# A conditioned two-layer decoder trunk on one core: the first phase with modulation columns by products that take the data as weights, and another order of its steps

## The chip, the cores and the metric

One Trainium2 chip, one of its cores. A core has engines that each work through their own queue in order and wait for one another by semaphores: TensorE (PE, with its weight loads shown apart as PEld), VectorE (DVE), ScalarE (ACT), GpSimd (POOL), and SyncE (SP), which here only issues DMAs. The metric is the device time of one execution in microseconds; the median of the runs counts.

## The reference, cut to what matters

Two layers; the first phase of the kernel computes the first lines of layer 0: the modulation of the six vectors `sh1 .. g2`, the norm, and the start of the q, k and v products.

```python
cond = jax.nn.silu(c)
for i in range(DEPTH):
    mod = cond @ ada_w[i] + ada_b[i]
    sh1, sc1, g1, sh2, sc2, g2 = [m[:, None, :] for m in jnp.split(mod, 6, axis=-1)]
    h = rms_norm(x, norm_mix[i]) * (1.0 + sc1) + sh1
    if i % N_MIXERS == 0:
        mix = stick_breaking_attention(h, sb_w_in[j], sb_w_out[j])   # qkv = h @ w_in, ...
    else:
        mix = dsa_attention(h, ...)
    x = x + g1 * mix
    h = rms_norm(x, norm_ffn[i]) * (1.0 + sc2) + sh2
    x = x + g2 * conv_ffn(h, ...)
```

D_MODEL is 1024, SEQ 512, BATCH 1, 16 heads of 64 in layer 0. All inputs are float32.

## The kernel before

Activations lie transposed: x and h are eight tiles of 128 features x 512 positions (f = 0 to 7). Each weight product keeps float32 accuracy by splitting both factors into a rounded high part and the rest (`whi`, `wlo` of a weight chunk by `split_hi` on ACT and `split_lo` on DVE; `hhi`, `hlo` of an h tile) and adding three products: hi x hi, weight-lo x hi, hi x lo (`mm3`, L257; PE lines L258 to L260). A weight chunk is 128 x 1024 floats (512 KB); `raws` has six buffers for chunks as they come from memory, and SP issues their loads in the order of the code, each when its buffer is free.

`stick_layer` (L539) begins with a phase written out by hand: the order of the lines in it is the order in each engine's queue. It has these steps.

- Loads: eight x tiles, the small constants `sm`, then for each f two chunks of the modulation weights (`load_ada`, scale first, then shift) between the weight chunks of the first q, k and v products (`FIRST`, L98; `fetch`).
- The norm: squares of the x tiles (ACT, one on DVE), DVE adds some of them, four products with `ones_mean` add over the partitions into `pt_norm` (L589). Then the inverse root on ACT (L679) and one Newton step on DVE (L687 to L689), which leave r.
- The modulation of tile f. For f below `ROWS` (5) `rows(f)` (L597) makes eight products with a 32-column tile of the condition as weights and the modulation weights as moving data (scale and shift together for f below `BOTH`, 3), ACT copies the sums (L608), and `columns(f)` (L610) turns them into columns by products with one moving column (L613). For the others `ada_dot` (L265) multiplies a chunk by the condition, spread over all partitions (`cond`), and sums along the row on DVE (`scale_dot`, `shift_dot`). `cond` comes as a 512 KB broadcast load (L693) and a Silu over it (L726).
- `factor(f)` (L626) adds the scale into `sfac`; `hi_part(f)` (L635) makes u = r * sfac * x on DVE and h's high part on ACT (u + shift); `lo_part(f)` (L640) makes the low part on DVE.
- The first products: `first_part(i, k)` (L661) adds h tile k into group i (q and k of head pairs 0 and 1, tiles `pt_first`), `first_v(k)` (L671) into the value groups (`pt_fv`).
- `keep_busy(n)` (L565) issues n products whose sums nobody reads.

After the last tile the q and k sums are copied out (`evac_q`, `evac_k`), and with `scores(0, 0)` (product z, L897) a second part begins in which a loop over heads is filled up with the products of the other chunks (`FILL`, L99).

Of the kernel before, what the change touches and what calls it, by code (L numbers as in the profile page):

```python
# [9 lines left out]
F32 = mybir.dt.float32  # L10
# [122 lines left out]
def kernel_body(ctx, tc, xT, wst, cst, smalls, crow, ccol, relb, outT):  # L133
# [405 lines left out]
    def stick_layer(l):  # L539
        with ExitStack() as st:  # L540
# [3 lines left out]
            head = ap.tile([P, 288], F32, name="head", bufs=1)  # L544
            condz, ccols, ghalf = head[:, :256], head[:, 256:256 + KT], head[:, 264:264 + KT]
            pool.memset(condz, 0.0)
# [3 lines left out]
            nc.sync.dma_start(sm, smalls)  # L550
# [11 lines left out]
            fetch(0)  # L562
            load_ada(1)
            fetch(1)
# [9 lines left out]
            act.activation(condz.rearrange("p (k m) -> p k m", m=32)[:, :, 0], ccols, AF.Silu)  # L574
# [5 lines left out]
            for f in range(KT):  # L580
                if f == 3:
                    dve.tensor_mul(sq[f], x[f], x[f])
                else:
                    act.activation(sq[f], x[f], AF.Square)
                if 2 < f < KT - 1:
                    dve.tensor_add(sq[2], sq[2], sq[f])
            warm(AF.Abs_reciprocal_sqrt)
            for i, f in enumerate((0, 1, KT - 1, 2)):
                pe.matmul(pn, lhsT=ones_mean, rhs=sq[f], start=i == 0, stop=i == 3)  # L589
                if i == 1:  # L590
                    keep_busy(4)
# [5 lines left out]
            def rows(f):  # L597

                pm = parts[f] = ptile([P, S], "pt_m", "tr")
                n = 2 * P if f < BOTH else P  # L600
                for k in range(KT):
                    q = k % 4
                    w = ada_raw[0 if f < BOTH and k >= 4 else 1, f]
                    kk = q if f < BOTH else k
                    pe.matmul(pm[32 * q:32 * q + 32, :n], lhsT=condz[:, 32 * k:32 * k + 32],
                              rhs=w[:, kk * n:(kk + 1) * n], start=k < 4, stop=k >= 4)
                pr = parts[f, "row"] = ap.tile([P, 2 * P], F32, name="pr", tag="m")
                act.activation(pr[:, :n], pm[:, :n], AF.Copy)  # L608

            def columns(f):  # L610
                pm, pr = parts[f], parts.pop((f, "row"))
                for i in range(2 if f < BOTH else 1):
                    pe.matmul(pm[:, 2 * P + i:2 * P + i + 1], lhsT=pr[:, i * P:(i + 1) * P], rhs=ones1, start=True, stop=True)  # L613
# [12 lines left out]
            def factor(f):  # L626

                src = mod[l][:, KT + f:KT + f + 1] if f >= ROWS else parts[f][:, 2 * P:2 * P + 1]
                dve.scalar_tensor_tensor(sfac[:, f:f + 1], src, ghalf[:, f:f + 1], sfac[:, f:f + 1], op0=OP.mult, op1=OP.add)
                if f < BOTH:  # L630
                    dve.tensor_add(mod[l][:, f:f + 1], parts[f][:, 2 * P + 1:2 * P + 2], shift_bias(f))
# [3 lines left out]
            def hi_part(f):  # L635
                us_[f] = ap.tile([P, S], F32, name="u", tag="ohi", bufs=6)
                dve.scalar_tensor_tensor(us_[f], r, sfac[:, f:f + 1], x[f], op0=OP.mult, op1=OP.mult)
                act.activation(hs[f][0], us_[f], AF.Identity, bias=mod[l][:, f:f + 1])

# [6 lines left out]
            def split_first(i):  # L646

                tag = ("at", "a")[i % 2]

                def new(name):  # L650
                    return ap.tile([P, LW], F32R, name=name, tag=tag)[:, :D] if i >= 4 else split_tile(name)

                split_hi(new, 0)
                yield
                split_lo(new)
                cs[i] = chunk(FIRST[i], 0)

            pts = [ptile([P, S], "pt_first", "mm" if i < 3 else "x") for i in range(4)]
            ptv = []

            def first_part(i, k):  # L661
                w = slice(k * P, (k + 1) * P)
                mm3(pts[i], cs[i][0][:, w], cs[i][1][:, w], hs[k][0], hs[k][1], k == 0, k == KT - 1)
# [7 lines left out]
            def first_v(k):  # L671
                if not ptv:
                    ptv.extend(ptile([P, S], "pt_fv", "z") for _ in range(2))
                whi, wlo = cs[4 + k // 4]
                for t in range(QT):
                    v_part(ptv, whi, wlo, k, t)
# [3 lines left out]
            rows(0)  # L680
            keep_busy(2)
            columns(0)
            keep_busy(6)
            s0, s1, s2, s3 = (split_first(i) for i in range(4))
            next(s0)
# [6 lines left out]
            row = crow[0:1, 0:1]  # L692
            nc.sync.dma_start(cond, bass.AP(tensor=row.tensor, offset=row.offset, ap=[[0, P], [1, D]]))  # L693
            factor(0)
            hi_part(0)
            rows(1)
            keep_busy(4)
            next(s0, None)
            load_ada(3)
            lo_part(0)  # L700
            columns(1)
            fetch(4)
            next(s1)
            first_part(0, 0)
            factor(1)
            hi_part(1)
            rows(2)
            next(s1, None)
            fetch(5)
            first_part(1, 0)  # L710
            lo_part(1)
            columns(2)
            next(s2)
            first_part(0, 1)
            first_part(1, 1)
            factor(2)
            hi_part(2)
            next(s2, None)
            lo_part(2)
            first_part(2, 0)  # L720
            first_part(2, 1)
            next(s3)
            next(s3, None)
            load_ada(4)
            nc.sync.dma_start(cons, cst)
            act.activation(cond, cond, AF.Silu)  # L726
            first_part(3, 0)
            first_part(3, 1)
            s4, s5 = split_first(4), split_first(5)
            first_part(0, 2)  # L730
            first_part(1, 2)
            rows(3)
            shift_dot(3)
            load_ada(5)
            next(s4)
            first_part(2, 2)
            columns(3)
            factor(3)
            hi_part(3)
            first_part(3, 2)  # L740
            next(s4, None)
            lo_part(3)
            rows(4)
            first_v(0)
            first_v(1)
            next(s5)
            next(s5, None)
            load_ada(6)
            shift_dot(4)
            load_ada(7)  # L750
            columns(4)
            first_part(0, 3)
            first_part(1, 3)
            for f in range(4, KT - 1):
                factor(f)
                hi_part(f)
                if f == 4:
                    first_part(2, 3)
                    first_part(3, 3)
                shift_dot(f + 1)  # L760
                lo_part(f)
                scale_dot(f + 1)
                if f == 4:
                    first_v(2)
                    first_v(3)
                if f < KT - 2:
                    for i in range(4):
                        first_part(i, f)
                    first_v(f)
            factor(KT - 1)  # L770
            hi_part(KT - 1)
            fetch(7)
            for i in range(2):
                first_part(i, KT - 2)
            lo_part(KT - 1)
# [45 lines left out]
            def evac_q(p, pt):  # L821
# [10 lines left out]
                later(0.8, lo)  # L832

            def evac_k(p, pt):
# [4 lines left out]
                def lo():  # L839
                    for e, t in enumerate(kd):  # L840
                        a = slice(64 * e, 64 * e + 64)
                        dve.tensor_sub(kl[e][a, :], pt[a, :], t[a, :].bitcast(F32))
# [5 lines left out]
                later(1.2, lo)  # L848
# [112 lines left out]
            for i in range(2):  # L961
# [3 lines left out]
            first_v(KT - 2)  # L965
            release(0.8)
            tick(1.4)
            first_v(KT - 1)
# [6 lines left out]
            for i in range(2, 4):  # L975
                first_part(i, KT - 2)
                first_part(i, KT - 1)
                tick(1.4)
            warm(AF.Sigmoid)
# [638 lines left out]
def _pack(i):  # L1618
# [6 lines left out]
    for t in range(ROWS):  # L1625
        if t < BOTH:
            both = np.concatenate([sc[t], sh[t]], axis=2)
            buf[CH["ada", 0, 1, t]] = both[:, :4].reshape(P, D)
            buf[CH["ada", 0, 0, t]] = both[:, 4:].reshape(P, D)
        else:  # L1630
            buf[CH["ada", 0, 1, t]] = sc[t].reshape(P, D)
# [80 lines left out]
```

## Time and profile before

| | us |
|---|---|
| median of 3 runs (lowest, highest) | 1260.68 (1260.23, 1261.4) |
| the profiled execution | 1260.67 |
| its span in the trace | 1258.9 |
| PE busy, share of the span | 1252.2 (99%) |
| DVE busy | 925.9 (74%) |
| ACT busy | 584.6 (46%) |

The times of a row in the timeline are its start and its length in microseconds from the start of the span; "x4" after a row means four instructions put together, and an fp32 product counts as two. What stands in brackets is how long the engine was idle before the row and what it waited for. A matmul's length includes its way through the array, so that neighbouring rows overlap; the distance of their starts is what they cost.

### The profile page before, as it was taken

The page shows a single profiled execution, that of the slowest core. Times are in us where ns is not written, and L with a number is a line of the kernel's source. Part 1 is how long each engine was busy: PE and PEld are TensorE (multiplying, and loading weights), DVE is VectorE, ACT ScalarE, POOL GpSimd, SP SyncE. Part 2 cuts the span into 40 slices and gives each one's busy share as a digit, 9 for nine tenths or more (in the row PEclk, how much of TensorE's full clock was granted, in tenths as well). Part 3 has the DMA queues.
Part 4 walks back from the last instruction along what each step waited for, and adds up shares of the span by engine and source line. Part 5 has one row for each costly group of instructions (what it writes and reads, how often), then busy time and mean ns, then how long its engine had stood idle before and what let it go on. Part 6 is the DMA issues. An engine that isn't in the chain of part 4 may idle for free.

```text
span 1258.9 us, 17379 instructions
## 1 busy us (share of the span) xinstructions
PE 1252.2 (99%) x6562; PEld 1038.0 (82%) x6562; DVE 925.9 (74%) x1573; ACT 584.6 (46%) x1029; POOL 66.1 (5%) x203
## 2 busy tenths in 40 slices
PE   9999999999999999999999999999999999999999
PEld 6888787798888888888887788887988888888887
DVE  5899998878877777885768878887876456456653
ACT  5477666554323423443445346656543234334330
POOL 0100000002000000000002350110000000000000
PEclk9999999999999999999999999999999999999999
DMA  9644444514575575554412222133122422433231
GB/s 376 217 138 133 130 133 141 170 33 141 191 255 189 179 239 192 187 183 155 130 34 68 84 76 75 52 101 105 64 92 75 134 92 68 125 90 95 76 92 67
DMA packets 49252, 163.05 MB, mean 130 GB/s; under 512 B 5632, under 2 KB 6144, under 8 KB 49168
## 3 DMA queue, kind: packets, MB, share of 16 engines
q1 hardware_dynamic: 48736, 161.15, 39.9%
q8 instruction: 52, 0.85, 0.3%
q10 hardware_dynamic: 432, 0.79, 0.2%
q14 instruction: 32, 0.26, 0.1%
HBM read 159.77 MB, written 2.14 MB: 129 GB/s over the span
## 4 chain that ended last, share of the span: by engine, by line
PE 97%; DMA 1%; DVE 1%; ACT 0%; issue 0%; SPq 0%; DVEq 0%
PE pt_u L259 12%; PE pt_u L258 12%; PE pt_u L260 12%; PE pt_d L259 5%; PE pt_d L258 5%; PE pt_d L260 5%; PE pt_l L258 2%; PE pt_q L258 2%; PE pt_l L259 2%; PE pt_l L260 2%; PE pt_q L260 2%; PE pt_q L259 2%; PE pt_first L258 2%; PE pt_first L260 2%; PE pt_first L259 2%; PE pt_qk L258 2%
## 5 line engine op out<-in xcount | busy, mean ns | idle before, releaser
L218 ACT ACTIVATE whi<-raw 128x1024 fp32r<-128x1024 f32 (+1 forms) x206 | 204.9, 1003 | 116.5 <-PE pt_d L260 86.3
L258 PE MATMUL pt_u<-hhi,whi 128*128 128x512 f32 x640 | 249.0, 389 | 0.0
L259 PE MATMUL pt_u<-hhi,wlo 128*128 128x512 f32 x640 | 249.0, 389 | 0.0
L260 PE MATMUL pt_u<-hlo,whi 128*128 128x512 f32 x640 | 249.0, 389 | 0.0
L226 DVE TENSOR_TENSOR wlo<-raw,whi 128x1024 fp32r<-128x1024 f32 (+1 forms) x194 | 223.4, 1154 | 10.0 <-ACT whi L218 9.2
L1031 ACT ACTIVATE y<-pt_u,sm 128x512 f32<-128x512 f32 x80 | 62.1, 777 | 190.6 <-PE pt_u L260 190.6
L258 PEld LDWEIGHTS pt_u<-hhi,whi 128*128 128x128 f32 x640 | 120.1, 188 | 25.0
L260 PEld LDWEIGHTS pt_u<-hlo,whi 128*128 128x128 f32 x640 | 120.1, 188 | 24.9
L259 PEld LDWEIGHTS pt_u<-hhi,wlo 128*128 128x128 f32 x640 | 120.1, 188 | 24.9
L1032 DVE SCALAR_TENSOR_TENSOR y<-pt_u,sm,y 128x511 f32<-128x511 f32 x80 | 59.9, 749 | 98.1 <-ACT y L1031 98.1
L258 PE MATMUL pt_d<-acthi,whi 128*128 128x512 f32 x288 | 112.0, 389 | 0.0
L259 PE MATMUL pt_d<-acthi,wlo 128*128 128x512 f32 x288 | 112.0, 389 | 0.0
L260 PE MATMUL pt_d<-actlo,whi 128*128 128x512 f32 x288 | 112.0, 389 | 0.0
L267 DVE SCALAR_TENSOR_TENSOR raw<-raw,cond 128x1024 f32<-128x1024 f32 x88 | 106.6, 1217 | 1.1 <-DMA raw<-wst 1.1
L385 DVE SCALAR_TENSOR_TENSOR x<-pt_d,mod,x 128x512 f32<-128x512 f32 x48 | 36.0, 750 | 72.8 <-PE pt_d L260 72.8
L242 ACT ACTIVATE acthi<-y 128x512 fp32r<-128x512 f32 x44 | 27.8, 632 | 104.7 <-DVE y L1050 104.7
L258 PE MATMUL pt_first<-hhi,whi 128*128 128x256 f32 (+1 forms) x200 | 64.1, 321 | 0.0
L259 PE MATMUL pt_first<-hhi,wlo 128*128 128x256 f32 (+1 forms) x200 | 62.9, 314 | 0.9 <-DVE wlo L226 0.8
L258 PEld LDWEIGHTS pt_d<-acthi,whi 128*128 128x128 f32 x288 | 54.1, 188 | 11.3
L260 PEld LDWEIGHTS pt_d<-actlo,whi 128*128 128x128 f32 x288 | 54.1, 188 | 11.2
L259 PEld LDWEIGHTS pt_d<-acthi,wlo 128*128 128x128 f32 x288 | 54.1, 188 | 11.2
L260 PE MATMUL pt_first<-hlo,whi 128*128 128x256 f32 (+1 forms) x200 | 63.1, 315 | 0.0
(256 smaller groups left out, 2512.4 us busy)
## 6 DMA issues: line engine op xcount, KB each, us to landing
raw<-wst SPq DMA_DIRECT2D x250, 512.0 KB, 3.7
raw<-wst SPq DMA_DIRECT2D x48, 384.0 KB, 3.0
th<-rb SPq DMA_DIRECT2D x16, 256.0 KB, 3.0
ada<-wst SPq DMA_DIRECT2D x4, 512.0 KB, 6.2
outT<-x SPq DMA_DIRECT2D x7, 256.0 KB, 2.0
x<-xT SPq DMA_DIRECT2D x5, 256.0 KB, 5.1
x<-xT ACTq DMA_DIRECT2D x3, 256.0 KB, 3.9
cond<-crow SPq DMA_DIRECT2D x1, 512.0 KB, 10.2
```

Source lines behind the costliest of these rows:

```text
L218: act.activation(hi[:, :n], raw[:, :n], AF.Copy)
L226: engine.tensor_sub(lo[:, :n], raw[:, :n], hi[:, :n].bitcast(F32))
L242: act.activation(hi, src, AF.Copy)
L258: pe.matmul(out, lhsT=whi, rhs=ahi, start=start, stop=False)
L259: pe.matmul(out, lhsT=wlo, rhs=ahi, start=False, stop=False)
L260: pe.matmul(out, lhsT=whi, rhs=alo, start=False, stop=stop)
L267: dve.scalar_tensor_tensor(raw, raw, 1.0, cond, op0=OP.mult, op1=OP.mult, accum_out=dst)
L385: dve.scalar_tensor_tensor(x[f][:, c], pt, mod[l][:, g * KT + f:g * KT + f + 1], x[f][:, c], op0=OP.mult, op1=OP.add)
L1031: act.activation(y, pt, AF.Identity, scale=cw[2], bias=sm[:, b + S_CB + c:b + S_CB + c + 1])
L1032: dve.scalar_tensor_tensor(y[:, 1:], pt[:, :S - 1], cw[1], y[:, 1:], op0=OP.mult, op1=OP.add)
```

## The change

Only the first phase changes. The core of the diff:

```diff
-FIRST = [("q", 0), ("k", 0), ("q", 1), ("k", 1), ("v", 0, 0), ("v", 0, 1)]
+FIRST = [("v", 0, 0), ("q", 0), ("k", 0), ("q", 1), ("k", 1), ("v", 0, 1)]
-BOTH = 3
-ROWS = 5
+ROWS = 3
...
-            nc.sync.dma_start(sm, smalls)
+            nc.sync.dma_start(sm[:, :S_CW], smalls[:, :S_CW])
+            nc.sync.dma_start(ident, cst[:, C_ID:C_ID + P])
...
             warm(AF.Silu)
-            act.activation(condz.rearrange("p (k m) -> p k m", m=32)[:, :, 0], ccols, AF.Silu)
+            act.activation(csilu, ccols, AF.Silu)
+            warm(AF.Abs_reciprocal_sqrt)
...
-            for i, f in enumerate((0, 1, KT - 1, 2)):
-                pe.matmul(pn, lhsT=ones_mean, rhs=sq[f], start=i == 0, stop=i == 3)
-                if i == 1:
-                    keep_busy(4)
+            def sum_tile(f):
+                pe.matmul(pn, lhsT=ones_mean, rhs=sq[f], start=f == 0, stop=f == 6)
...
+            dve.tensor_tensor(cond.rearrange("p (k m) -> p k m", k=KT), ident[:, None, :].to_broadcast([P, KT, P]),
+                              csilu[:, :, None].to_broadcast([P, KT, P]), op=OP.mult)
...
+            def column(f, g):
+                pm = parts[f, g] = ptile([P, S], "pt_m", "tr")
                 for k in range(KT):
-                    q = k % 4
-                    w = ada_raw[0 if f < BOTH and k >= 4 else 1, f]
-                    kk = q if f < BOTH else k
-                    pe.matmul(pm[32 * q:32 * q + 32, :n], lhsT=condz[:, 32 * k:32 * k + 32],
-                              rhs=w[:, kk * n:(kk + 1) * n], start=k < 4, stop=k >= 4)
+                    pe.matmul(pm[:, :1], lhsT=ada_raw[g, f][:, k * P:(k + 1) * P], rhs=csilu[:, k:k + 1],
+                              start=k == 0, stop=k == KT - 1)
...
+            def shift(f):
+                dve.tensor_add(mod[l][:, f:f + 1], parts[f, 0][:, :1], shift_bias(f))
...
+            def xr_part(f):
+                us_[f] = ap.tile([P, S], F32, name="xr", tag="olo" if f < 6 else "ohi", bufs=6)
+                dve.tensor_mul(us_[f], r, x[f])
+            def hi_both(f):
+                for out in (hs[f][0], us_[f]):
+                    act.activation(out, us_[f], AF.Identity, scale=sfac[:, f:f + 1], bias=mod[l][:, f:f + 1])
+            def lo_sub(f):
+                dve.tensor_sub(hs[f][1], us_.pop(f), hs[f][0].bitcast(F32))
+            def cond_spread():
+                for i in range(2):
+                    cond_pt.append(ptile([P, S], "pt_c", "mm"))
+                    pe.matmul(cond_pt[i], lhsT=ones_mean, rhs=cond[:, i * S:(i + 1) * S], start=True, stop=True)
+            def cond_copy(i):
+                act.activation(cond[:, i * S:(i + 1) * S], cond_pt[i], AF.Copy, scale=float(D))
...
-            rows(0)
-            keep_busy(2)
-            columns(0)
-            keep_busy(6)
...
+            column(0, 1)
+            column(0, 0)
+            cond_spread()
...
-            row = crow[0:1, 0:1]
-            nc.sync.dma_start(cond, bass.AP(tensor=row.tensor, offset=row.offset, ap=[[0, P], [1, D]]))
...
-            act.activation(cond, cond, AF.Silu)
...
-            rows(3)
...
-            rows(4)
...
+            scale_dot(3)
+            lo_sub(2)
...
+            scale_dot(4)
+            xr_part(5)
+            lo_sub(3)
...
-            for i in range(2):
-                first_part(i, KT - 1)
-                later(0.1, lambda i=i: (evac_k if i else evac_q)(0, pts[i]))
-                tick(0.7)
+            first_part(0, KT - 1)
+            evac_q(0, pts[0], True)
+            first_part(1, KT - 1)
+            evac_k(0, pts[1], True)
```

So for tiles 0 to 2 the scale and the shift each come from a `column`: eight products that take a chunk of the modulation weights as stationary data and one column of the condition as moving data. The scales of tiles 3 and 4 come from dots on DVE. `cond` is made on the chip: DVE spreads the condition over a diagonal, two products with `ones_mean` sum it over the partitions into `pt_c`, ACT copies it out. From tile 2 on h is r * x on DVE, then two ACT passes (high part, and the same unrounded), then one subtraction on DVE. The value chunk comes first, the chunk of the next value group is split within the loop, the table loads of the inverse root and of the sigmoid stand earlier, and the idle products behind the first ten are gone.

On PE, from the norm to the first weight product. Before (`pt_idle` is what `keep_busy` writes, `pt_m` the modulation sums, `head` and `ecols` hold the condition and a column of ones, `pr` is ACT's copy of the sums):

```order
L589 MATMUL pt_norm<-sq,ones_mean 128x512 x2
L570 MATMUL pt_idle<-ones_mean 128x128 x4
L589 MATMUL pt_norm<-sq,ones_mean 128x512 x2
L605 MATMUL pt_m<-ada,head 32x256 x8
L570 MATMUL pt_idle<-ones_mean 128x128 x2
L613 MATMUL pt_m<-ecols,pr 128x1 x2
L570 MATMUL pt_idle<-ones_mean 128x128 x6
L605 MATMUL pt_m<-raw,head 32x256 x8
L570 MATMUL pt_idle<-ones_mean 128x128 x4
L613 MATMUL pt_m<-ecols,pr 128x1 x2
L258 MATMUL pt_first<-hhi,whi 128x512
```

Now, on the same engine from the same place (`pt_c` is the spread condition, `pt_fv` the value sums):

```order
L587 MATMUL pt_norm<-sq,ones_mean 128x512 x6
L616 MATMUL pt_m<-head,ada 128x1 x16
L663 MATMUL pt_c<-cond,ones_mean 128x512 x2
L714 MATMUL pt_fv<-whi,hhi 128x256 x4
L616 MATMUL pt_m<-head,raw 128x1 x16
L714 MATMUL pt_fv<-wlo,hhi 128x256 x4
L714 MATMUL pt_fv<-whi,hlo 128x256 x4
L698 MATMUL pt_first<-hhi,whi 128x512
```

Two columns of tile 0 and the spread now stand ahead of the first weight product, and the columns of tile 1 behind the first four value products; the rows of tile 1 stood ahead of all weight products before.

On DVE, from the Newton step to the second u. Before (`sfac` is the factor of one tile, `mod` its shift):

```order
L689 SCALAR_TENSOR_TENSOR r<-t,r 128x512
L629 SCALAR_TENSOR_TENSOR sfac<-pt_m,head,sfac 128x1
L631 TENSOR_TENSOR mod_87<-pt_m,sm 128x1
L637 SCALAR_TENSOR_TENSOR u<-r,sfac,x_90 128x512
L226 TENSOR_TENSOR wlo<-raw,whi 128x1024
L641 SCALAR_TENSOR_TENSOR hlo<-u,mod_87,hhi 128x512
L629 SCALAR_TENSOR_TENSOR sfac<-pt_m,head,sfac 128x1
L631 TENSOR_TENSOR mod_87<-pt_m,sm 128x1
L637 SCALAR_TENSOR_TENSOR u<-r,sfac,x_91 128x512
```

Now:

```order
L728 SCALAR_TENSOR_TENSOR r<-t,r 128x512
L633 SCALAR_TENSOR_TENSOR sfac<-pt_m,head,sfac 128x1
L636 TENSOR_TENSOR mod_87<-pt_m,sm 128x1
L642 SCALAR_TENSOR_TENSOR u<-r,sfac,x_90 128x512
L225 TENSOR_TENSOR wlo<-raw,whi 128x1024
L669 SCALAR_TENSOR_TENSOR hlo<-u,mod_87,hhi 128x512
L649 TENSOR_TENSOR xr<-r,x_92 128x512
L633 SCALAR_TENSOR_TENSOR sfac<-pt_m,head,sfac 128x1
L642 SCALAR_TENSOR_TENSOR u<-r,sfac,x_91 128x512
L636 TENSOR_TENSOR mod_87<-pt_m,sm 128x1
```

For tile 0 the order is the same, with the shift ahead of u; for tile 1 u has moved ahead of the shift, and r * x of tile 2 ahead of both.

On DVE, one step of the loop over the later tiles. Before:

```order
L267 SCALAR_TENSOR_TENSOR raw,mod_87<-raw,cond 128x1024
L621 TENSOR_TENSOR mod_87<-mod_87,sm 128x1
L641 SCALAR_TENSOR_TENSOR hlo<-u,mod_87,hhi 128x512
L267 SCALAR_TENSOR_TENSOR raw,mod_87<-raw,cond 128x1024
L629 SCALAR_TENSOR_TENSOR sfac<-mod_87,head,sfac 128x1
L637 SCALAR_TENSOR_TENSOR u<-r,sfac,x_95 128x512
```

Now:

```order
L266 SCALAR_TENSOR_TENSOR raw,mod_87<-raw,cond 128x1024
L625 TENSOR_TENSOR mod_87<-mod_87,sm 128x1
L633 SCALAR_TENSOR_TENSOR sfac<-mod_87,head,sfac 128x1
L266 SCALAR_TENSOR_TENSOR raw,mod_87<-raw,cond 128x1024
L649 TENSOR_TENSOR xr<-r,x_96 128x512
L656 TENSOR_TENSOR hlo<-xr,hhi 128x512
```

The factor stands directly behind its shift, the scale dot that follows it is that of the next tile, and u, which needed the factor, has become r * x, which needs none.

More of the change, by code (lines that the diff above doesn't have):

```diff
@@ L655, in split_first, with value_tile, first_part @@
                 split_lo(new)
-                cs[i] = chunk(FIRST[i], 0)
-            pts = [ptile([P, S], "pt_first", "mm" if i < 3 else "x") for i in range(4)]
+                cs[i] = chunk(key, 0)
+            def value_tile(h, name):
+                return ap.tile([P, LW], F32R, name=name, tag=("at", "a")[h])[:, :D]
+            pts = {}
             ptv = []
-            def first_part(i, k):
+            def first_part(i, k, n=range(3)):
                 w = slice(k * P, (k + 1) * P)
-                mm3(pts[i], cs[i][0][:, w], cs[i][1][:, w], hs[k][0], hs[k][1], k == 0, k == KT - 1)
+                if i not in pts:
+                    pts[i] = ptile([P, S], "pt_first", "mm" if i < 3 else "x")
+                whi, wlo = cs[i + 1]
+                for j in n:
+                    pe.matmul(pts[i], lhsT=(wlo if j == 1 else whi)[:, w], rhs=hs[k][1 if j == 2 else 0],
+                              start=k == 0 and j == 0, stop=k == KT - 1 and j == 2)
             def v_part(out, whi, wlo, k, t):
@@ L691, in stick_layer @@
             fetch(3)
-            row = crow[0:1, 0:1]
-            nc.sync.dma_start(cond, bass.AP(tensor=row.tensor, offset=row.offset, ap=[[0, P], [1, D]]))
             factor(0)
+            shift(0)
+            u_part(0)
+            next(sp[0], None)
             hi_part(0)
-            rows(1)
-            keep_busy(4)
-            next(s0, None)
-            load_ada(3)
[L700 to L704, printed above, removed]
@@ L725, in stick_layer @@
-            nc.sync.dma_start(cons, cst)
-            act.activation(cond, cond, AF.Silu)
[L727 to L730, printed above, removed]
+            fetch(4)
+            lo_part(0)
+            first_v(0, (0,))
+            column(1, 1)
+            next(sp[1])
+            xr_part(2)
+            factor(1)
+            column(1, 0)
+            u_part(1)
+            first_v(0, (1,))
+            shift(1)
@@ new lines, in stick_layer @@
+            hi_part(1)
+            next(sp[1], None)
+            load_ada(3)
+            first_v(0, (2,))
+            first_part(0, 0, (0, 2))
+            lo_part(1)
+            xr_part(3)
+            next(sp[2])
+            first_v(1, (0,))
+            column(2, 1)
+            cond_copy(0)
+            first_part(0, 0, (1,))
+            first_v(1, (1,))
+            factor(2)
+            cond_copy(1)
+            next(sp[2], None)
+            load_ada(4)
+            column(2, 0)
@@ new lines, in stick_layer @@
+            next(sp[3])
+            first_v(1, (2,))
+            xr_part(4)
+            shift(2)
+            hi_both(2)
+            first_part(0, 1, (0, 2, 1))
+            next(sp[3], None)
+            fetch(5)
+            scale_dot(3)
+            lo_sub(2)
+            next(sp[4])
+            for k in range(2):
+                first_part(1, k)
+            shift_dot(3)
+            first_part(0, 2, (0, 1))
+            first_v(2)
+            first_part(0, 2, (2,))
+            factor(3)
@@ L747, in stick_layer @@
[L747 to L759, printed above, removed]
-                shift_dot(f + 1)
[L761 to L766, printed above, removed]
+            nc.sync.dma_start(sm[:, S_CW:], smalls[:, S_CW:])
@@ L847, in evac_k @@
                     act.activation(t[b, :], pt[a, :], AF.Copy)
-                later(1.2, lo)
+                    if now:
+                        lo(e)
+                if not now:
+                    later(1.2, lambda: (lo(0), lo(1)))
             def qk_steps(p):
@@ L1625, in _pack @@
     for t in range(ROWS):
[L1626 to L1631, printed above, removed]
+        buf[CH["ada", 0, 1, t]] = sc[t].reshape(P, D)
+        buf[CH["ada", 0, 0, t]] = sh[t].reshape(P, D)
     w = f["sb_w_in"][0]
```

167 lines of the change are left out of this document (83 added, 84 removed).

## The prediction

> **What bounds the kernel now.** Read first: the page's busy line, then the busy time of each engine in stretches cut at the first weight product (17.77 us), at the last wait before the stream runs without a gap (32.50) and at the first score product (57.88).
>
> ```profile
> span 1258.9 us, 17379 instructions
> PE 1252.2 (99%) x6562; PEld 1038.0 (82%) x6562; DVE 925.9 (74%) x1573; ACT 584.6 (46%) x1029; POOL 66.1 (5%) x203
> ```
>
> ```profile
> 0.00:17.77 17.77, 16.12 (x101) 11.48 (x101) 8.68 (x18) 10.97 (x18) 0.96 (x6) 1.00 0.90 349
> 17.77:32.50 14.73, 13.12 (x95) 8.37 (x94) 10.39 (x18) 8.83 (x13) 0.07 (x1) 1.00 1.03 410
> 32.50:57.88 25.38, 25.38 (x156) 22.82 (x157) 20.79 (x37) 9.61 (x14) 3.18 (x13) 1.00 0.66 216
> 57.88:1258.90 1201.02, 1197.54 (x6215) 995.32 (x6213) 886.07 (x1502) 555.21 (x987) 61.85 (x184) 1.00 0.38 121
> ```
>
> Columns of the stretches: length, then busy time of PE, weight loads, DVE, ACT, POOL, then granted clock, DMA share, GB/s. PE is the bound: it is idle for 3.5 us in the 1201 us after 57.88 and for nothing between 32.50 and 57.88. Code after the first scores is the same in both kernels, so whatever moves that point moves the end by as much. The whole question is **when PE starts the first score product**, now 57.88. The ends of that phase in PE's timeline, and one full step of the loop over tiles (four `pt_first` groups, one `pt_fv` group):
>
> ```profile
> 17.77 0.48 PE L258 MATMUL pt_first<-hhi,whi 128*128 128x512 f32 x1
> 45.27 0.39 PE L258 MATMUL pt_first<-hhi,whi 128*128 128x512 f32 x1
> 49.47 0.39 PE L258 MATMUL pt_first<-hhi,whi 128*128 128x512 f32 x1
> 57.88 0.23 PE L897 MATMUL z<-kd,qs 128*128 128x128 f32 x1
> ```
>
> A step takes 49.47 - 45.27 = 4.20 us, eight of them 33.6. From 17.77 to 57.88 there are 40.1, so 6.5 us are not weight products: `rows`, `columns` and waits. These weight products are the same in the new kernel, only in another order. The new end is therefore the new start of the products, plus 33.6, plus what else PE must do or wait for in between.
>
> **What one pass costs on PE.** An fp32 product is two passes in the trace (x4 is two products).
>
> ```profile
> 1.03 4.64 PE L570 MATMUL pt_idle<-ones_mean 128*128 128x128 f32 x20 [1.03 <-DVE ecols L158]
> 5.55 2.68 PE L589 MATMUL pt_norm<-sq,ones_mean 128*128 128x512 f32 x4
> 8.06 1.05 PE L570 MATMUL pt_idle<-ones_mean 128*128 128x128 f32 x8
> 10.21 1.45 PE L589 MATMUL pt_norm<-sq,ones_mean 128*128 128x512 f32 x3
> 11.59 1.07 PE L605 MATMUL pt_m<-ada,head 128*32 128x256 f32 x16
> 13.16 0.52 PEld L613 LDWEIGHTS pt_m<-ecols,pr 128*128 128x128 f32 x4
> 13.60 0.19 PEld L570 LDWEIGHTS pt_idle<-ones_mean 128*128 128x128 f32 x1
> ```
>
> Passes with 128 weight columns and one moving column (L613) start (13.60 - 13.16)/4 = 0.11 us apart, as idle passes with 128 moving columns do, 1.05/8 with their tail left in: the weight load sets the pace. So one `column`, 8 products or 16 passes, is **1.78 us** (16 x 0.1115). A 512-column pass is (1.45 - 0.59)/2 = 0.43 us, its last 0.59 being its own length.
>
> **Part 1, the norm (to 11.6).** Four fp32 products become six (12 passes), the four idle products between them go, and the table load moves ahead of the squares.
>
> ```profile
> 3.52 0.20 ACT L574 ACTIVATE head<-head 128x8 f32<-128x8 f32 x1
> 4.87 1.15 ACT L584 ACTIVATE sq<-x 128x512 f32<-128x512 f32 x2 [1.14 <-DMA x<-xT]
> 9.64 1.28 ACT L400 ACT_TABLE_LOAD   x1
> ```
>
> The load of 1.28 now stands behind 3.52, so the first square starts near 5.03, not 4.87, and the first pass near 5.71. The first two passes run slow as in the row at 5.55 and bring PE to about 7.29; ten more at 0.43 end at 11.58. The old phase reached its first modulation product at 11.59: **no gain**. PE's own queue takes the place of the squares and the table load as what is late.
>
> **Part 2, start of the products.** Column (0,scale) runs 11.58 to 13.36, (0,shift) to 15.15, the two `pt_c` products (4 passes x 0.43) to 16.87.
>
> ```profile
> 13.86 0.69 DVE L689 SCALAR_TENSOR_TENSOR r<-t,r 128x512 f32<-128x512 f32 x1
> 14.47 0.21 DVE L629 SCALAR_TENSOR_TENSOR sfac<-pt_m,head,sfac 128x1 f32<-128x1 f32 x1
> 14.60 0.15 DVE L631 TENSOR_TENSOR mod<-pt_m,sm 128x1 f32<-128x1 f32 x1
> 14.72 0.75 DVE L637 SCALAR_TENSOR_TENSOR u<-r,sfac,x 128x512 f32<-128x512 f32 x1
> 15.51 0.72 ACT L638 ACTIVATE hhi<-u,mod 128x512 fp32r<-128x512 f32 x1 [1.19 <-DVE u L637]
> 17.54 0.36 PE L613 MATMUL pt_m<-ecols,pr 128*128 128x1 f32 x2
> 18.01 0.22 DVE L629 SCALAR_TENSOR_TENSOR sfac<-pt_m,head,sfac 128x1 f32<-128x1 f32 x1 [0.74 <-PE pt_m L613]
> ```
>
> `factor(0)` still comes behind r, near 14.5. But `shift(0)` stands ahead of `u_part(0)` on DVE and waits for the second column: its last pass ends 0.17 behind its 0.11 slot, and DVE follows 0.11 later (18.01 behind 17.54 + 0.36 below). 15.15 + 0.28 is 15.42, then u 15.54 to 16.29, hi 16.33 to 17.05, first product at **17.10**, or 17.20 with the 0.1 by which a first pass is longer (0.48 at 17.77, 0.39 at 45.27). Queued behind that waiting shift are u, the first lo copy and `lo_part(0)`; all are paid in the 17.10. Against 17.77 this gains 0.6 us, since idle products, `rows(1)`, its ACT copy and `columns(1)` no longer stand ahead.
>
> **Part 3, inside the stream.** Four more columns: 4 x 1.78 = **7.1 us** on PE, where the old kernel lost 6.5 to its rows, columns and waits. No row shows sixteen one-column passes in a stretch; between one pass at the 32-column spacing (1.07/16 = 0.07, tail included) and one cold pass (4.64/20 = 0.23) the four would be 4.5 to 15 us. I take 1.78, since L613 has the same 128x128 weights and one moving column. End: 17.20 + 33.6 + 7.1 = **57.9**, if PE waits nowhere else. That equals the old 57.88.
>
> **Does PE wait?** The nearest thing is hi(1): `shift(1)` follows column (1,shift) by 0.28, hi is there 1.24 us after that column, and PE has eight value products and two `pt_first` products to do, 0.95 + 0.46 = 1.41. Slack 0.2. Then DVE, whose steady step is here:
>
> ```profile
> 37.95 0.74 DVE L641 SCALAR_TENSOR_TENSOR hlo<-u,mod,hhi 128x512 fp32r<-128x512 f32 x1
> 38.61 1.22 DVE L267 SCALAR_TENSOR_TENSOR raw<-raw,cond 128x1024 f32<-128x1024 f32 x1
> 39.87 0.22 DVE L629 SCALAR_TENSOR_TENSOR sfac<-mod,head,sfac 128x1 f32<-128x1 f32 x1
> 40.13 0.75 DVE L637 SCALAR_TENSOR_TENSOR u<-r,sfac,x 128x512 f32<-128x512 f32 x1
> 40.80 1.22 DVE L267 SCALAR_TENSOR_TENSOR raw<-raw,cond 128x1024 f32<-128x1024 f32 x1
> 42.13 0.74 DVE L641 SCALAR_TENSOR_TENSOR hlo<-u,mod,hhi 128x512 fp32r<-128x512 f32 x1
> 31.23 1.22 DVE L226 TENSOR_TENSOR wlo<-raw,whi 128x1024 fp32r<-128x1024 f32 x1
> 32.36 0.74 DVE L641 SCALAR_TENSOR_TENSOR hlo<-u,mod,hhi 128x512 fp32r<-128x512 f32 x1
> ```
>
> A dot is 1.26, a lo copy 1.13, a 512-wide operation 0.6 to 0.67. The old step was 42.13 - 37.95 = 4.18, as long as PE's 4.20. The new one holds two dots, factor, xr and the subtraction: 1.26 + 1.26 + 0.2 + 0.6 + 0.6 = 3.9, and 5.05 where a lo copy is in it. DVE is busy without a pause from `shift(2)` on (27.7, behind the last column), with two dots that were rows on PE before. Its instructions laid end to end give lo(2) at 30.9, lo(3) 35.9, lo(4) 41.0, lo(5) 44.9, lo(6) 48.4 and lo(7) 51.7. PE, laid out the same way, asks for them at 31.4, 37.4, 41.6, 45.8, 50.0 and 53.5. All are early, the nearest by 0.5; without that cover each us that DVE is late is a us of PE. ACT makes two outputs of 0.61 each from tile 2 on; it was busy 9.61 of the last 25.38 us and takes 3.7 more there. The old Silu of cond with its table load, off PE's path, goes; two copies of 0.6 replace it.
>
> **DMA.** The queue moved 410 GB/s, a 512 KB tile each 1.28 us. The 512 KB broadcast of cond goes, the constants come in pieces. The nearest need is the second column:
>
> ```profile
> 12.00 0.17 PEld L605 LDWEIGHTS pt_m<-ada,head 128*32 128x32 f32 x8 [0.26 <-DMA ada<-wst]
> 15.84 0.16 PEld L605 LDWEIGHTS pt_m<-raw,head 128*32 128x32 f32 x8 [0.54 <-DMA raw<-wst]
> ```
>
> Those tiles were there at 12.00 and 15.84; now they stand behind fewer bytes, or one chunk more (1.28), and are asked for at 13.36 and 19.5. Later loads wait for buffers as before, some 2 us ahead of their dots. Nothing is on the path. The q and k copies made at once are likewise covered:
>
> ```profile
> 51.76 1.20 ACT L831 ACTIVATE qs<-pt_first 64x512 fp32r<-64x512 f32 x2 [1.75 <-PE pt_first L260]
> 55.42 1.41 DVE L842 TENSOR_TENSOR kz<-pt_first,kd 64x512 fp32r<-64x512 f32 x2 [1.02 <-ACT kd L847]
> ```
>
> The last `pt_first` group of q ends near 53.9; z needs four ACT copies of 0.6 and one kz subtraction of 0.7 behind it, near 57.0.
>
> **Sum.** The profiled execution took 1260.67 for a span of 1258.9, 1.8 outside it, and equals the median 1260.68 of the runs shown. 57.9 against 57.88 leaves **1260.7**.
>
> **Rivals.** (a) *The columns overlap* and cost half: `rows` passes of 32 columns do start closer. Six columns save 5.3 us, of which r's own end holds back 1; the rest, 4.3, gives 1256.4. Against it: L613's spacing. Chance 0.04. (b) *DVE is late*: should its work from 27.7 to lo(4), 13.3 us, stretch by 10%, PE waits 0.8 us at lo(4), and perhaps again; 1261 to 1262.5. For it: slacks of 0.2 and 0.5 are thin; against it, the old step shows DVE at this pace without a pause. Chance 0.15. (c) *The clock falls, and the kernel is slower.* The sixteen idle products go, and twice (11.6 to 15.2, 17.7 to 21.3) PE does 3.57 us of passes with one moving column. The row at 1.03 shows passes at half speed, and the row at 5.55 that it lasted until about 7; the granted clock reads 1.00 there too, so only spacing tells. Half speed costs half of each us: one such phase of 6 us after each stretch makes 1263.7 to 1266.7; it decides from 5 us of slow time. Against it: no slow pass later in the old trace, though there no more than four one-column passes stood in a row. Chance 0.06. [...] (d) *The change doesn't do what it says*, columns and dots coming later than the plan puts them: then PE waits as in (b).
>
> **How the numbers follow.** Forecast as summed: 0.72. Left open: 0.03, mostly waits over 2.5 us. 0.2% is 2.5 us, about what a measurement of this kernel can tell from no change. Faster: 0.04 by (a). Slower: (c) and most of the open rest, 0.09. Within: 0.87. Without any wait PE would end 0.3 earlier, an earlier full clock gives another 0.4, and runs lie 0.5 below their median: low 1259.5. High takes in (b): 1262.7. That leaves out (a) and (c).
>
> **What would show it.** Right: column passes 0.11 apart, first value product near 17.1, no PE gap over 0.3 us after it, z near 57.9, the stretch after it 1201 us as before. Wrong: passes at 0.2 us after 15 or 21 us (c); PE waiting for hlo (b); columns under 1.2 us (a); z below 57, which the sum of PE's own work excludes.

## The result, and the profile after

The changed kernel is **slower**: 1269.32 us in the median of 4 runs (1267.48 to 1274.01) against 1260.77 of the kernel before in the same measurement (4 runs, 1260.23 to 1261.4). The ratio is 1.0075, 95% interval 1.0063 to 1.0087. The time lies outside the predicted range, on the slow side. The profiled execution is the fastest of the four, 1267.48 with a span of 1265.7, so as before 1.8 us lie outside the span.

The page of the changed kernel, its span, its busy line and the clock row of its 40 slices:

```profile
span 1265.7 us, 17323 instructions
...
PE 1259.7 (100%) x6538; PEld 1047.4 (83%) x6538; DVE 927.0 (73%) x1577; ACT 586.2 (46%) x1029; POOL 65.4 (5%) x202
...
PEclk8999999999999999999999999999999999999999
```

PE is busier than before, by 7.5 us, with 24 instructions fewer. It doesn't wait longer; its instructions take longer. The page gives it away in one digit: the first slice of the clock row is 8. To see where, the span is cut wherever the granted clock changes. The columns are those of the stretches in the prediction; the last but two is the clock:

```profile
4.80:15.04 10.24, 9.74 (x50) 6.36 (x49) 6.62 (x13) 5.63 (x10) 2.38 (x5) 1.00 1.04 398
15.04:18.46 3.42, 3.42 (x8) 1.71 (x7) 2.99 (x4) 1.67 (x2) 0.00 (x0) 0.50 1.02 408
18.46:21.87 3.41, 3.41 (x33) 3.41 (x32) 0.97 (x2) 0.00 (x0) 0.00 (x0) 1.00 1.03 411
21.87:25.28 3.41, 3.41 (x15) 3.22 (x16) 2.57 (x4) 2.69 (x5) 0.00 (x0) 0.50 0.95 333
25.28:28.70 3.42, 3.42 (x32) 3.38 (x30) 1.25 (x2) 0.89 (x1) 0.00 (x0) 1.00 0.52 180
28.70:35.52 6.82, 6.82 (x24) 6.00 (x24) 5.28 (x12) 2.63 (x4) 0.00 (x0) 0.50 0.55 167
35.52:64.71 29.19, 28.11 (x157) 24.23 (x155) 21.40 (x39) 15.70 (x22) 0.41 (x8) 1.00 0.69 241
64.71:1265.70 1200.99, 1197.57 (x6214) 995.31 (x6214) 885.73 (x1502) 554.37 (x985) 61.85 (x184) 1.00 0.38 121
```

Three things are to be seen. The first score product z starts at 64.71, 6.83 later than the old 57.88, and the stretch behind it takes 1200.99, where the old one took 1201.02: the whole difference of the spans, 6.8, arises ahead of z. The clock is at half for four pieces of 3.41 us (the last two are joined), 13.65 us in all. And PE is busy through all of them: it doesn't pause there, it runs at half speed. From 15.04 to z the one stretch with an idle PE is the last, 29.19 with 28.11 busy.

What PE did before each half-speed piece, from its timeline in the changed kernel:

```profile
11.12 3.63 PE L616 MATMUL pt_m<-head,ada 128*128 128x1 f32 x32
14.61 3.35 PE L663 MATMUL pt_c<-cond,ones_mean 128*128 128x512 f32 x4
16.98 1.74 PE L714 MATMUL pt_fv<-whi,hhi 128*128 128x256 f32 x4
18.56 3.80 PE L616 MATMUL pt_m<-head,raw 128*128 128x1 f32 x32
22.22 1.20 PE L714 MATMUL pt_fv<-wlo,hhi 128*128 128x256 f32 x4
23.22 1.05 PE L714 MATMUL pt_fv<-whi,hlo 128*128 128x256 f32 x4
...
25.57 1.84 PE L616 MATMUL pt_m<-head,ada 128*128 128x1 f32 x16
27.27 0.48 PE L698 MATMUL pt_first<-hhi,wlo 128*128 128x512 f32 x1
27.59 0.63 PE L714 MATMUL pt_fv<-wlo,hhi 128*128 128x256 f32 x4
28.05 2.82 PE L616 MATMUL pt_m<-head,ada 128*128 128x1 f32 x16
30.73 1.20 PE L714 MATMUL pt_fv<-whi,hlo 128*128 128x256 f32 x4
```

The two columns of tile 0 fill 11.12 to 14.61 and half speed begins at 15.04; those of tile 1 fill 18.56 to 22.22, and it begins at 21.87; those of tile 2 stand from 25.57 to 30.73, and half speed lasts from 28.70 to 35.52. The four value products at 22.22 need 1.00 to the next row, where the prediction has 0.95 for eight. Each half-speed piece of 3.41 us follows a piece of the same length that was mostly passes with **one moving column** (2.98, 3.31, 2.35 and 2.03 us of it, by the starts of the rows; 28.70 to 35.52 taken as two halves). That is a coincidence in time so far; the runs below make it a cause.

On top of the clock, 1.24 us are a wait at the end, from the timeline of ACT and PE:

```profile
62.84 0.59 ACT L895 ACTIVATE kd<-pt_first 64x512 fp32r<-64x512 f32 x1 [0.97 <-DVE kz L891]
...
63.24 0.40 PE L698 MATMUL pt_first<-hlo,whi 128*128 128x512 f32 x1
63.44 0.59 ACT L896 ACTIVATE kd<-pt_first 64x512 fp32r<-64x512 f32 x1
64.06 0.60 ACT L1023 ACTIVATE vs<-pt_fv 128x512 f32<-128x512 f32 x1
...
64.71 0.33 PE L949 MATMUL z<-kd,qs 128*128 128x128 f32 x1 [1.08 <-ACT vs L1023]
```

z writes into the bank that held the first half of the value sums. ACT frees it with the copy `vs`, and that copy stands in ACT's queue behind the four k copies (`kd`), the third of which waits 0.97 us for DVE. PE could have gone on at 63.47 (0.23 behind its last product) and goes on at 64.71.

### The profile page after: what moved, and what is told of

It is laid out like the page before. It is cut to its first block, busy times and chain, and to the rows that moved or that the text cites. A ratio compares the mean times of both kernels' runs of the same rounds, so it can differ in the third digit from the quotient of the medians.

```text
span 1265.7 us, 17323 instructions
## 1 busy us (share of the span) xinstructions
PE 1259.7 (100%) x6538; PEld 1047.4 (83%) x6538; DVE 927.0 (73%) x1577; ACT 586.2 (46%) x1029; POOL 65.4 (5%) x202
## 4 chain that ended last, share of the span: by engine, by line
PE 98%; DVE 1%; ACT 1%; issue 0%; ACTq 0%; DVEq 0%
PE pt_u L257 11%; PE pt_u L258 11%; PE pt_u L259 11%; PE pt_d L257 5%; PE pt_d L258 5%; PE pt_d L259 5%; PE pt_q L257 2%; PE pt_l L257 2%; PE pt_l L259 2%; PE pt_l L258 2%; PE pt_q L259 2%; PE pt_q L258 2%; PE pt_first L257 2%; PE pt_first L259 2%; PE pt_first L258 2%; PE pt_qk L257 2%
## 5 line engine op out<-in xcount | busy, mean ns | idle before, releaser
L1082 DVE SCALAR_TENSOR_TENSOR y<-pt_u,sm,y 128x510 f32<-128x510 f32 x80 | 59.9, 749 | 2.8
L963 DVE TENSOR_TENSOR_SCAN m<-m,below 128x127 f32<-128x127 f32 (+1 forms) x64 | 52.2, 816 | 3.2 <-ACT m L957 3.1
L242 DVE TENSOR_TENSOR actlo<-y,acthi 128x512 fp32r<-128x512 f32 x44 | 30.5, 693 | 30.7 <-ACT acthi L241 30.7
```

The lines of the kernel that those rows point to most:

```text
L242: dve.tensor_sub(lo, src, hi.bitcast(F32))
L963: dve.tensor_tensor_scan(rev, rev, below[:, S - ns:S - 1][:, ::-1], 0.0, OP.mult, OP.add)
L1082: dve.scalar_tensor_tensor(y[:, 2:], pt[:, :S - 2], cw[0], y[:, 2:], op0=OP.mult, op1=OP.add)
```

## The experiments

Two theories for the 6.8 us, and one rival. **Clock theory**: stretches of passes with one moving column bring the clock down, though PE is busy; about 5.7 us. **Bank theory** (of z): z's wait for its bank, 1.2 us. **Rival**: the change costs that time in another way, by the columns' weight loads or by the sixteen idle products that it takes out, and the clock only follows. What the expectations below say on how the clock is set is their author's assumption; the traces show the granted clock alone.

### The same columns, 128 moving columns wide

Each of the changed kernel's column products gets the same vector 128 times as moving data, so that weight loads, passes and their places stay and only the width differs.

```diff
-                    pe.matmul(pm[:, :1], lhsT=ada_raw[g, f][:, k * P:(k + 1) * P], rhs=csilu[:, k:k + 1],
+                    pe.matmul(pm[:, :128], lhsT=ada_raw[g, f][:, k * P:(k + 1) * P], rhs=csilu[:, k:k + 1].to_broadcast([P, 128]),
```

> The changed kernel with the moving operand of every column product 128 columns wide (the condition's column repeated 128 times); weights, count of passes and order stay. Theory G (stretches of one-column passes count as idle for the clock gate): no window of half clock after 7 us, passes 0.1115 us apart throughout, first score product near 58.2 to 59.5 (64.71 less the 5.7 us lost to half clock, with what is left of the wait of 1.2 us for the bank of z), time 1261 to 1262.5. Rival N (the clock falls because the idle products behind the first ten are gone): the windows of half clock stay, time near 1269. Rival W (the weight load itself sets the clock off): the same, near 1269.

Measured: 1261.37 us (1261.23 to 1262.73, 10 runs) beside 1260.27 of the kernel before; ratio 1.0009, interval 1.0000 to 1.0019. Eight of the 8.5 us are gone in the median, and z comes at 58.61 instead of 64.71: in the profiled executions the clock costs 6.1 us. Stretches, then PE's timeline, of this run:

```profile
5.02:17.11 12.09, 11.70 (x56) 7.21 (x55) 8.61 (x15) 6.75 (x11) 2.36 (x5) 1.00 1.04 402
17.11:20.84 3.73, 3.73 (x36) 3.73 (x35) 2.01 (x4) 0.34 (x1) 0.00 (x0) 1.00 1.04 413
20.84:57.36 36.52, 36.52 (x221) 32.31 (x219) 29.86 (x54) 20.71 (x28) 0.41 (x8) 1.00 0.81 282
```

```profile
11.13 3.73 PE L616 MATMUL pt_m<-head,ada 128*128 128x128 f32 x32
14.71 1.88 PE L663 MATMUL pt_c<-cond,ones_mean 128*128 128x512 f32 x4
16.56 0.74 PE L714 MATMUL pt_fv<-whi,hhi 128*128 128x256 f32 x4
...
57.13 0.40 PE L698 MATMUL pt_first<-hlo,whi 128*128 128x512 f32 x1
58.61 0.33 PE L949 MATMUL z<-kd,qs 128*128 128x128 f32 x1 [1.08 <-ACT vs L1023]
```

The clock is full throughout, and 32 passes take nearly the same time as with one column (3.58 from 11.13 to 14.71, against 3.49): 127 columns more cost 0.09 us. The idle products are missing here too, so their absence alone isn't the cause in this kernel. PE is busy for 36.52 of the 36.52 us from 20.84 on: at full speed DVE, ACT and the loads keep up with it. The wait for `vs` is unchanged at 1.08. The clock theory holds, the rival falls.

### How many moving columns are enough

The same edit with 32 and with 64 in the place of 128, one run each.

> The changed kernel with 32 moving columns in each column product: a pass still takes 0.1115 us, so about an eighth as much moving work for the same time as a 256-column stream. If the gate looks at whether PE is issuing at all, 32 columns behave like 1 and half-clock windows stay (1267 to 1270). If it looks at the share of cycles in which data moves, 32 columns are 12% of them: I expect that still counts as idle, 1266 to 1270; above some share the loss goes to nothing, 1261 to 1262.

> As the last, with 64 moving columns, 24% of the cycles. It places the share between idle and busy: full clock and 1261 to 1262 if it lies below a quarter, half-clock windows and 1266 to 1270 if above.

Measured: 1264.24 with 32 columns, 1261.13 with 64. Stretches of the run with 32, then of the one with 64:

```profile
5.00:14.98 9.98, 9.46 (x48) 6.08 (x47) 6.56 (x13) 5.42 (x10) 2.41 (x5) 1.00 1.02 385
14.98:18.40 3.42, 3.42 (x7) 1.63 (x6) 3.06 (x4) 1.67 (x2) 0.00 (x0) 0.50 1.03 414
18.40:21.81 3.41, 3.41 (x34) 3.41 (x32) 0.97 (x2) 0.00 (x0) 0.00 (x0) 1.00 1.03 411
21.81:25.23 3.42, 3.42 (x16) 3.23 (x16) 2.57 (x4) 2.58 (x5) 0.00 (x0) 0.50 1.00 362
25.23:58.00 32.77, 32.77 (x197) 29.09 (x197) 25.70 (x48) 16.80 (x22) 0.00 (x0) 1.00 0.78 269
```

```profile
5.00:20.00 15.00, 14.20 (x80) 9.97 (x80) 10.57 (x18) 7.08 (x12) 3.43 (x5) 1.00 1.04 402
20.00:58.00 38.00, 37.42 (x227) 33.05 (x226) 30.01 (x55) 21.43 (x29) 0.41 (x8) 1.00 0.80 281
```

With 32 columns the two dense stretches still lose the clock, for one piece each; the looser columns of tile 2, with weight products between them, no longer do. The time lies between the two outcomes that were expected for 32 columns. With 64 nothing is lost, as expected if the border lies below 64. Nor, by the author's estimate, was that a matter of where the pieces fell. After the start of full speed (4.16 in the clock records of this run's trace) its clock doesn't change, so no piece shows; in the changed kernel all changes from 4.80 to 35.52 lie whole steps of 3.41 us apart. Counted in such steps from 4.16, one goes from 10.99 to 14.40, and in it PE starts 30 passes of 64 columns and no others (in the run with 32 columns the same passes fill 11.11 to 14.60). In dense stretches of passes 0.11 us apart the border is therefore between 32 and 64 columns, by one run on each side. The count of passes or of weight loads is the same in all of these kernels.

What exactly counts is not shown. It isn't simply the sum of the moving columns: that piece of the 64-column run, if it lies where the estimate puts it, sums up to 1920 and kept full speed, while the piece from 25.28 to 28.70 of the changed kernel, 23 passes of 1, six of 256 and one of 512, sums up to 2071 and was followed by half speed.

### The old kernel without its idle products

The sixteen idle products that the change removes, taken out of the kernel before.

```diff
-                if i == 1:
-                    keep_busy(4)
...
-            keep_busy(2)
...
-            keep_busy(6)
...
-            keep_busy(4)
```

> The kernel before without the idle products behind the first ten (4, 2, 6 and 4 of them). Theory G: the phase has gaps but still matrix work in every 3.41 us window, so the clock stays full or loses one window at most, 1260 to 1262.5. Rival N: half clock in two to four windows between 12 and 30 us, 1264 to 1268.

Measured: 1262.47 in one run, span 1260.7, 1.8 more than the profiled kernel before. Stretches:

```profile
7.00:16.41 9.41, 5.67 (x42) 1.82 (x40) 7.05 (x14) 6.53 (x10) 0.00 (x0) 1.00 1.03 409
16.41:23.23 6.82, 6.34 (x33) 3.80 (x29) 3.43 (x6) 3.49 (x5) 0.00 (x0) 0.50 1.02 415
23.23:58.00 34.77, 33.58 (x218) 28.23 (x218) 26.69 (x48) 14.36 (x20) 3.63 (x13) 1.00 0.77 266
```

Here PE really pauses (5.67 of 9.41 us busy; in the last 3.41 of them 1.70, by passes with 32 weight columns or one moving column), and the clock falls for two pieces of 3.41 us. The clock theory had allowed one such piece at most, on the assumption that matrix work in every 3.41 us holds the clock, which fails here (1.70 us of it did not); the rival had allowed two to four; the time lies at the upper end of what the clock theory had given and below the rival's 1264. The span grows by 1.8, less than the 3.4 that half of 6.82 makes; what offsets the rest was not followed up. So the idle products of the old kernel did help to hold the clock, worth some 2 us by this one run, and the rival has this much for it: without them a PE that pauses loses the clock too. In the changed kernel PE doesn't pause.

### One column against 128, by themselves

To the kernel before, 32 products with x tiles as weights are added ahead of z, their sums unused: once with one moving column, once with 128.

```diff
+            du = ptile([P, S], "pt_du", "tr")
+            for k in range(32):
+                pe.matmul(du[:, :1], lhsT=x[k % KT][:, :P], rhs=ccols[:, k % KT:k % KT + 1], start=True, stop=True)
```

```diff
+                pe.matmul(du[:, :128], lhsT=x[k % KT][:, :P], rhs=x[(k + 1) % KT][:, P:2 * P], start=True, stop=True)
```

> The kernel before with 32 products added ahead of the first score product (64 passes, tiles of x as weights, one moving column; their sums are not used). Theory G: 7.1 us for the passes at full clock, and one or two windows of 3.41 us at half clock in or behind them, 1.7 to 3.4 us more: 1269.5 to 1271.5. Rival N (no idle product is missing here): 7.1 us and no half clock, 1267.9.

> As the last one, with 128 moving columns in place of one. Both theories: 64 passes of 0.1115 us, 7.1 us, no half clock, 1267.9. Rival W (many fp32 weight loads in a row lower the clock): as with one column, 1269.5 to 1271.5.

Measured: 1273.69 (span 1271.9) with one column, 1267.24 (span 1265.5) with 128. The narrow run's stretches and timeline, then the wide run's timeline:

```profile
57.40:60.61 3.21, 3.21 (x30) 3.17 (x30) 2.10 (x3) 1.58 (x3) 0.00 (x0) 1.00 0.53 158
60.61:64.02 3.41, 3.41 (x18) 3.41 (x18) 0.00 (x0) 0.00 (x0) 0.00 (x0) 0.50 0.55 159
64.02:67.43 3.41, 3.41 (x17) 3.41 (x18) 0.00 (x0) 0.00 (x0) 0.00 (x0) 0.50 0.00 0
67.43:74.27 6.84, 6.84 (x33) 6.84 (x34) 2.13 (x5) 1.97 (x6) 0.00 (x0) 0.50 0.00 1
```

```profile
57.47 10.77 PE L987 MATMUL pt_du<-head,x 128*128 128x1 f32 x64
68.09 0.45 PE L897 MATMUL z<-kd,qs 128*128 128x128 f32 x1
```

```profile
57.32 7.30 PE L987 MATMUL pt_du<-x,x 128*128 128x128 f32 x64
64.38 0.30 PE L897 MATMUL z<-kd,qs 128*128 128x128 f32 x1
```

In the narrow run the clock is full for the first 3.2 us, then half. 64 passes take 10.62 us to z; the wide ones take 7.06, the 7.1 that the spacing of 0.11 gives. The weight loads and their place in the queue are the same, the kernel before has its idle products, and PE waits for nothing: the moving operand alone takes the clock away. (Here it differs in its values as well as in its width; in the 128-column run it was the same vector.) The narrow run pays 6.4 us of span more, near the 6.8 that half of its 13.65 us at half speed makes. It is also 2 us above what was expected of it: one or two pieces at half speed were reckoned with, and there are four. As the passes take longer at half speed, two more pieces of 3.41 us hold nothing else, and each of these is followed by half speed too. The last piece, from 70.85 to 74.27, holds no narrow pass and follows one that had 0.66 us of them, then score and value products at half speed. Why half speed went on there isn't settled by these runs; in the changed kernel full speed came back at 25.28 after a similar piece (0.35 us of narrow passes, then value and `pt_first` products).

### The wait for the bank

In the kernel with 128 columns, the last value products and the copy `vs` are put ahead of the last k group and its copies.

```diff
             first_part(0, KT - 1)
             evac_q(0, pts[0], True)
-            first_part(1, KT - 1)
-            evac_k(0, pts[1], True)
-            tick(1.4)
-            first_part(2, KT - 1)
             first_v(KT - 1)
...
             act.activation(vrow[:, :S], ptv[0], AF.Copy)
+            first_part(1, KT - 1)
+            evac_k(0, pts[1], True)
             dve.tensor_copy(vrow[:, S:], ptv[1])
```

> The 128-column form, and the last value products with ACT's copy of their first bank put ahead of the last k group and its copies, so that the bank which the first score product needs comes free earlier. Theory Z (the 1.25 us ahead of z is the wait for that bank, behind the k copies on ACT): no wait ahead of z, z at 57.3 to 57.6, time 1.0 to 1.2 us under the 128-column form, about 0.3 to 0.5 under the kernel before. Rival (z waits for the k copies themselves): z within 0.4 us of 58.6, no gain.

Measured: 1261.37 (1261.17 to 1262.75, 11 runs) against 1260.43; ratio 1.0007, interval 0.9998 to 1.0016. That is no gain over the 1261.37 without the reordering. The timeline shows why:

```profile
57.47 0.22 PE L949 MATMUL z<-kd,qs 128*128 128x128 f32 x1
57.57 0.59 ACT L895 ACTIVATE kd<-pt_first 64x512 fp32r<-64x512 f32 x1 [0.75 <-DVE kz L891]
...
58.80 0.69 DVE L891 TENSOR_TENSOR kz<-pt_first,kd 64x512 fp32r<-64x512 f32 x1 [1.26 <-ACT kd L896]
...
59.64 0.36 PE L257 MATMUL pt_v<-whi,hhi 128*128 128x256 f32 x1 [0.90 <-DVE kz L891]
```

z no longer waits: it comes at 57.47, right behind the last product, so the bank theory's mechanism is right. But after six more value products PE needs the bank of the k sums for the next value chunk, and that is free only behind the last `kz`. A new wait of the same size has taken the place of the old. The chain behind both is the k copies, done one head after the other (ACT, DVE, ACT, DVE); between the k group and z only three `pt_first` groups are left here, 2.0 us of PE (55.43 to 57.47 in the timeline), where the kernel before had four of them and the last two value groups as well, 5.6 us (52.24 to 57.88).

### The new order with the old rows

The last run takes the new order of chunks and tiles 0 to 2 by the old `rows` and `columns` (their weights packed as before, no one-column stretch longer than four passes), eight idle products behind the first columns, and the reordered end.

```diff
-            column(0, 1)
-            column(0, 0)
+            rows(0)
             cond_spread()
+            columns(0)
+            keep_busy(8)
...
-            column(1, 1)
+            rows(1)
...
-            column(1, 0)
...
             first_v(0, (1,))
+            columns(1)
```

> The new order with the old modulation of tiles 0 to 2 (rows of 32 weight columns and 256 moving columns, ACT's copy, columns by two products) in place of the six columns, eight idle products behind the first of them, and the earlier copy of the value bank. Theory C (with the clock mended, the columns' weight loads are what the new order still pays: 1.78 us each against about 0.7 for a tile's half of rows and columns): first score product near 54, time 1256 to 1257.5, below both kernels. Rival D (DVE and the loads set the end once PE has room): z at 56.5 or later, 1259 to 1260.5.

Measured: 1259.03 (1258.8 to 1260.85, 11 runs) against 1260.43; ratio 0.9988, interval 0.9979 to 0.9997. It is faster than both kernels, by 1.4 us or 0.1% over the one before, with the clock full from the start of the products on. PE's timeline at the end:

```profile
55.76 0.22 PE L962 MATMUL z<-kd,qs 128*128 128x128 f32 x1
...
56.76 0.28 PE L259 MATMUL pt_v<-wlo,hhi 128*128 128x256 f32 x1
57.93 0.36 PE L257 MATMUL pt_v<-whi,hhi 128*128 128x256 f32 x1 [0.90 <-DVE kz L904]
```

The time is the one that rival D had given, and z lies between what theory C and rival D had put it at (near 54, and 56.5 or later). z comes 2.1 us earlier than in the kernel before, and the wait for the k copies gives 1.1 of it back (57.93 where 56.88 was due, 0.12 behind the product before). With enough PE work behind the k group that 1.1 should come too; this wasn't tried. The run changes several things at once (rows, idle products, the end), so it doesn't say what each is worth.

## Why the prediction was wrong, point by point

**The frame** held: the stretch behind z is 1200.99 against 1201.02, so z decides, and 1.8 us lie outside the span.

**Part 1 (norm ends 11.58, no gain)**: the first column pass came at 11.12. In this execution the norm's twelve passes took 5.31 us from 5.81 on, 0.44 each, so all of them ran at full speed; in the old one the clock was full only near 7 (its first four passes took 2.68 from 5.55). The prediction had put that down as a possible 0.4. Right but for that.

**Part 2 (first value product at 17.10)**: 16.98, by two errors that cancel. The columns ran at 0.109 a pass, as forecast; but the two `pt_c` products began 0.54 early and then ran at half speed from 15.04 on.

**Part 3 (four more columns, 7.1 us; z at 57.9)** is where it failed. The price that it chose, "I take 1.78, since L613 has the same 128x128 weights and one moving column", was right for PE's queue: the run with 128 columns, at full clock, takes 40.8 us from its first value product (16.56) to the end of its products (57.36), where the sum has 33.6 + 7.1 = 40.7. The step that failed is that the sum put what such a stretch does to the clock at nothing, and left it to rival (c) with a chance of 0.06: it takes every product among and behind the columns at full speed, and only a wait ("if PE waits nowhere else") could make it longer. From the first value product to the last product takes 46.5 us here (16.98 to 63.47) instead of 17.2 to 57.9, 40.7: 5.8 more. Of the 13.65 us at half speed 11.7 lie in this stretch, and half of that is 5.85.

**Rival (c)** was the right mechanism: clock, cause and the place "after 15 or 21 us" are as it said. Its price and its chance were wrong. It reckoned with one slow phase of up to 6 us behind each of two stretches at most; there were four pieces of 3.41 us, since tile 2's columns, too, brought the clock down (they were spread, but 2.35 of the 3.42 us from 25.28 on were narrow passes) and their second half then ran slow and kept it down. The chance of 0.06 rested on "no slow pass later in the old trace, though there no more than four one-column passes stood in a row". The second half of that sentence cancels the first: the old trace held no case that could have shown it, so it was no evidence against. From 4.80 to 35.52 every piece between two changes of the granted clock is 3.41 or 3.42 us long, or two or three times that. With weights, passes and their order the same, in these runs the width of the moving operand decided (13.65 us at half speed with one column, none with 128), in a PE that the trace shows as fully busy (3.41 of the 3.41 us from 18.46 on, with half speed behind them).

**"Does PE wait?"**: in the stream it does not, also at full clock (36.52 of 36.52 us). No wait for DVE or a load shows there, so the slacks of 0.2 and 0.5 held and rival (b) did not occur.

**"The q and k copies made at once are likewise covered"** was wrong by 1.2 us. The sum counted the operands of z (four ACT copies and one `kz`) and not the bank it writes, which a copy queued behind those on ACT sets free. At full clock, too, z waited 1.08 there.

**Sum**: with the columns widened, so with full clock and this wait, the change takes 1261.37, within 0.7 us of the forecast, in part because two errors offset each other: the products end 0.5 earlier than 57.9, and z waits 1.25 behind them. What the forecast missed by 8.6 us in the median is nearly all the clock. The four runs of the changed kernel differ by their mean granted clock: 0.995 at 1267.48, 0.993 at 1269.14 and 1269.5, 0.989 at 1274.01. (1 - clock) times the span is 6.3, 8.9 and 14.0 us lost, each to within 0.6 as the clock is given to three digits; the trace of the first has 13.65 us at half speed, so 6.8. At 1.71 us for a piece that is, as an estimate, 4, 5, 5 and 8 pieces, and the times lie 1.7, 2.0 and 6.5 us above the fastest, as one, one and four pieces more would put them (1.7 and 6.8). So the number of half-speed pieces seems to vary from run to run, with the profiled run the lowest of the four; where they lie in the other runs was not traced.

## What to carry to other kernels

A stretch of products with few moving columns costs its passes on PE's queue, 0.11 us each here, and then it may cost the clock (some 5.85 us here between the first value product and the last product). A PE that is busy all the time is no proof of full speed (6.82 of 6.82 us busy here at a clock of 0.50): look at the granted clock piece by piece, and at how wide the passes in the 3.4 us ahead of a slow piece are. Where they are narrow, widen the moving operand, which was nearly free here up to 128 columns (32 passes took 3.58 us against 3.49, and the kernel 1261.4 us against 1269.3). When a trace holds no case of what a change introduces, its silence on that point is no evidence, and the rival keeps its weight. A product waits for the bank it writes as well as for its operands (z 1.08 us for `vs` here): when copies move, look for what is queued behind them, and for the next product that needs their bank.

## What the runs showed of the hardware that was not expected

- A PE that the trace shows as busy without a gap can be granted half the clock: passes with 1 moving column, 0.11 us apart, bring it down for the next 3.41 us (18.46 to 21.87 of the changed kernel busy throughout, then 0.50 to 25.28); with 32 columns in dense stretches too (0.50 from 14.98 to 18.40 and from 21.81 to 25.23); with 64 and 128 not (1.00 from 5.00 to 58.00 and from 5.02 to 57.36; one run each with 32 and 64).
- Half speed can outlast the narrow passes: 10.62 us of them were followed by 6.1 us more at half (68.09 to 74.21), in score and value products of 128 and 256 columns. The last 3.4 us of this are unexplained.
- The same kernel lost some 6.8 to 14.0 us to it in different executions, by their mean granted clock, so that its fastest run understates the cost by 1.8 us against the median.
